# MLP and FFN up products by Strassen's seven products, down products over 512 features at a time

## The chip, the cores and the metric

One core of one Trainium2 chip runs the whole program: 512 tokens, 1024 features, all data and products in 32 bits. The metric is the device time of one execution in microseconds (us). The engines are TensorE (PE, its weight loads apart as PEld), VectorE (DVE), ScalarE (ACT), GpSimd (POOL) and SyncE (SP, which here issues the DMAs). Each runs its own instructions in a fixed order and waits on semaphores for the others. Products end up in PSUM, in banks of 128 x 512; everything else lies in SBUF.

## The reference

Two layers of a first block, then one layer of a second. What the change touches are the two feed-forward parts; attention, convolution and mLSTM parts stay as they are.

```
# first block, for l in 0, 1 (hidden 4096)
u = rmsnorm(x, norm_mlp[l])
x = x + square(relu(u @ w_mlp_up[l])) @ w_mlp_down[l]
# second block, once (hidden 2816)
h = modulate(rms_norm(x, g_ffn), sh_f, sc_f)
x = x + gt_f * ((silu(h @ w_gate) * (h @ w_up)) @ w_down)
```

The vector `mod` (shifts, scales, gates) is a product of `w_ada` with one vector; the kernel computes it on DVE during layer 1's MLP.

## The kernel before

All activations lie transposed: eight tiles `x[j]` of 128 features x 512 tokens. A product is made to nearly full 32-bit precision out of three matmuls of type fp32r: every weight and activation is split into a high part (`hi`, a cast on ACT) and a low part (`lo`, a subtraction on DVE), and hi x hi, hi x lo and lo x hi add up in one PSUM bank (L230, L231, L232).

`Prog` (L48) holds the program as a list: a "unit" is a piece of weights of 128 x 4 x 256 (`split`, L164: ACT's cast L171, DVE's subtraction L172), a "do" is anything else, "bg" is background work of which `rate` pieces follow each unit. A unit's split is written two units ahead of its matmuls. The tile layer then orders each engine's instructions by its own estimate of times, so that rows of neighbouring steps mix. The pools `whp` (4 buffers each for `wh` and `wl`), `rawp` (3 buffers of 1 MB for weights as they come), `gp` (60 slots of 128 x 512, tag g) and `mmp` (4 PSUM banks, tag mm) set when a buffer comes free.

`linear` (L188) makes four output tiles from weights of 1024 x 512: for each unit, for each of its two tiles, 4 x 3 matmuls of 512 columns (tokens); at `parts_=2` twice as many of 256 columns. After the last one `evac` reads the bank: L732 (relu and scale on DVE), L733 (square on ACT) and `hilo` (L285, L286) for an up tile, L740 (addition to x) for a down tile.

In each layer's MLP `up(c)` makes 1024 of 4096 hidden features and `down(c)` takes them back, in the order up 0, up 1, down 0, up 2, down 1, up 3, down 2, down 3. Ahead of it, `evmix` (L715) adds each tile of the mixing product to x and `prep` (L289) makes the tile's `hi` and `lo`. In layer 1 the 96 ada products (L803, DVE, on SBUF data) are background work. `fin` (L881) makes the next norm for the first half of the tokens while the second part of the last down group runs. In the FFN `gateup(c, g)` makes two gate and two up tiles together (L1315 to L1317), eleven times, and `down(c)` takes 1024 features. `hnorm` (L843) makes its normed input, half the tokens at a time.

## Time and profile before

| | us |
|---|---|
| median of 3 runs | 2070.45 |
| lowest, highest | 2070.16, 2070.49 |
| the profiled execution | 2069.96 |
| its span | 2067.9 |

| engine | busy, share of the span | instructions |
|---|---|---|
| PE | 2057.1 us, 99% | 9944 |
| DVE | 1260.0 us, 61% | 2245 |
| ACT | 845.6 us, 41% | 1359 |
| POOL | 19.7 us, 1% | 33 |

The profile is of one execution. The span runs from its first instruction to its last; the time outside it belongs to the execution too. Matmuls overlap, so a busy PE says that something was always in it, not how fast; their pace is read from start to start. An average over the whole span hides that the stages have different loads: layer 0's MLP lies at about 325 to 715 us, layer 1's at 1040 to 1435, the FFN from 1690 to the end.

### The profile page before, as it was taken

The numbers are of one execution on the slowest core, as the hardware profiler recorded it, in microseconds if no ns is written. First come the engines' busy times: TensorE is split into PE (matmuls) and PEld (weight loads), VectorE is DVE, ScalarE is ACT, GpSimd is POOL, SyncE is SP. The second block draws the span as 40 slices with busy tenths as digits, with TensorE's granted clock in tenths as the row PEclk, the third lists the DMA queues.
The fourth block names the chain that finished last, engine by engine and source line by source line (L and its number), as shares of the span: only waits on it lengthen the run. The fifth ranks groups of instructions, "written<-read, shape, count | busy, mean of one in ns | idle before, by whom it ended". The sixth has DMA issues, their size and how long they took to land.

```text
span 2067.9 us, 25080 instructions
## 1 busy us (share of the span) xinstructions
PE 2057.1 (99%) x9944; PEld 1700.7 (82%) x9944; DVE 1260.0 (61%) x2245; ACT 845.6 (41%) x1359; POOL 19.7 (1%) x33
## 2 busy tenths in 40 slices
...
GB/s 204 102 94 93 79 62 102 82 102 102 96 88 102 87 94 90 102 102 62 62 123 169 209 141 194 145 195 98 82 82 62 42 81 103 81 103 101 83 111 51
DMA packets 122148, 215.25 MB, mean 104 GB/s; under 512 B 5808, under 2 KB 30640, under 8 KB 122032
## 3 DMA queue, kind: packets, MB, share of 16 engines
...
## 4 chain that ended last, share of the span: by engine, by line
PE 97%; DVE 1%; ACT 1%; issue 0%; DMA 0%; POOL 0%; SPq 0%; POOLq 0%; DVEq 0%; ACTq 0%
PE mm L230 25%; PE mm L232 25%; PE mm L231 25%; PE mm L1315 4%; PE mm L1317 4%; PE mm L1316 4%; PE at L352 1%; PE mm L260 1%; PE mm L261 1%; PE mm L262 1%; PE ot L386 1%; PE at L371 1%; PE at L1188 0%; PE at L1196 0%; PE at L582 0%
## 5 line engine op out<-in xcount | busy, mean ns | idle before, releaser
L230 PE MATMUL mm<-g,wh 128*128 128x512 f32 (+1 forms) x2400 | 919.5, 384 | 1.0 <-ACT wh L171 0.8
L232 PE MATMUL mm<-g,wl 128*128 128x512 f32 (+1 forms) x2400 | 916.0, 382 | 0.0
L231 PE MATMUL mm<-g,wh 128*128 128x512 f32 (+1 forms) x2400 | 915.4, 382 | 0.0
L171 ACT CAST wh<-raw 128x1024 fp32r<-128x1024 f32 (+2 forms) x356 | 366.4, 1032 | 825.8 <-PE mm L231 648.6
L172 DVE TENSOR_TENSOR wl<-raw,wh 128x1024 fp32r<-128x1024 f32 (+2 forms) x356 | 424.9, 1195 | 448.1 <-ACT wh L171 445.8
L230 PEld LDWEIGHTS mm<-g,wh 128*128 128x128 f32 x2400 | 450.4, 188 | 90.5 <-issue 4.3
L231 PEld LDWEIGHTS mm<-g,wh 128*128 128x128 f32 x2400 | 450.6, 188 | 86.3 <-issue 1.2
L232 PEld LDWEIGHTS mm<-g,wl 128*128 128x128 f32 x2400 | 450.7, 188 | 86.1
L1317 PE MATMUL mm<-g,wl 128*128 128x512 f32 (+1 forms) x384 | 142.6, 372 | 0.0
L1316 PE MATMUL mm<-g,wh 128*128 128x512 f32 (+1 forms) x384 | 142.4, 372 | 0.0
L1315 PE MATMUL mm<-g,wh 128*128 128x512 f32 (+1 forms) x384 | 142.2, 372 | 0.0
L286 DVE TENSOR_TENSOR g<-g,g 128x512 fp32r<-128x512 f32 x96 | 66.4, 691 | 49.7 <-ACT g L285 49.2
L285 ACT CAST g<-g 128x512 fp32r<-128x512 f32 x96 | 59.6, 621 | 60.6 <-DVE g L707 26.6
L1317 PEld LDWEIGHTS mm<-g,wl 128*128 128x128 f32 x384 | 72.3, 188 | 12.6
L1316 PEld LDWEIGHTS mm<-g,wh 128*128 128x128 f32 x384 | 72.3, 188 | 12.5
L1315 PEld LDWEIGHTS mm<-g,wh 128*128 128x128 f32 x384 | 72.1, 188 | 12.4
L740 DVE TENSOR_TENSOR x<-mm,x 128x512 f32<-128x512 f32 (+1 forms) x68 | 44.8, 658 | 56.5 <-PE mm L232 56.5
L803 DVE SCALAR_TENSOR_TENSOR g<-g,g 128x512 f32<-128x512 f32 x96 | 63.8, 688 | 8.6 <-DMA g<-w_ada 8.5
L733 ACT ACTIVATE g<-g 128x512 f32<-128x512 f32 x64 | 40.3, 630 | 70.1 <-DVE g L732 70.1
L360 ACT ACTIVATE g<-g,nm 128x128 f32<-128x128 f32 (+3 forms) x96 | 53.2, 555 | 17.8 <-DVE nm L355 17.1
L601 DVE MAX8 m<-g 128x8 f32<-128x256 f32 (+2 forms) x96 | 53.3, 558 | 1.9
L602 DVE MATCH_REPLACE8 g<-m,g 128x256 f32<-128x256 f32 (+2 forms) x96 | 52.1, 543 | 0.0
...
## 6 DMA issues: line engine op xcount, KB each, us to landing
raw<-w_in SPq DMA_DIRECT2D x53, 1024.0 KB, 5.0
raw<-w_mlp_up SPq DMA_DIRECT2D x32, 1024.0 KB, 5.4
raw<-w_mlp_down SPq DMA_DIRECT2D x32, 1024.0 KB, 5.1
...
raw<-w_gate SPq DMA_DIRECT2D x11, 1024.0 KB, 5.1
raw<-w_up SPq DMA_DIRECT2D x11, 1024.0 KB, 5.2
raw<-w_down SPq DMA_DIRECT2D x10, 1024.0 KB, 5.0
raw<-w_mix_out SPq DMA_DIRECT2D x8, 1024.0 KB, 5.1
```

Of the source, the lines that this page charges most:

```text
L171: act.copy(hi, raw)
L172: dve.tensor_sub(lo, raw, hi.bitcast(F32))
L230: pe.matmul(ps, wh, hi[:, cs], start=st, stop=False)
L231: pe.matmul(ps, wh, lo[:, cs], start=False, stop=False)
L232: S["pe"] = pe.matmul(ps, wl, hi[:, cs], start=False, stop=en)
L285: act.copy(hi, src)
L286: dve.tensor_sub(lo, src, hi.bitcast(F32))
L601: dve.max(m8, acc[i][:, :W_])
L803: dve.scalar_tensor_tensor(w, w, 1.0, S["cb", n2], op0=ALU.mult, op1=ALU.mult, accum_out=modp[:, n2, n : n + 1])
L1315: pe.matmul(ps, wh, hi[:, cs], start=s == 0 and k_ == 0, stop=False)
L1316: pe.matmul(ps, wh, lo[:, cs], start=False, stop=False)
L1317: pe.matmul(ps, wl, hi[:, cs], start=False, stop=s == 1 and k_ == 3)
```

## The change

A unit of four output tiles (two column halves of 256, called 0 and 1) is now made by `strassen`. It halves K (tiles 0 to 3 and 4 to 7), the columns and the tokens, and makes seven products of half-size matrices in place of eight. Each is a unit of 128 x 4 x 256 weights with 2 x 4 x 3 matmuls of 256 columns. They add up in four banks, X, Z, Y and V, and additions out of the banks put them together (`keep`, `e11` to `e21`); X, Z and V are read while later products still go into them. Sums and differences of weights (tag ws, a new pool of 3 buffers) are made on GpSimd by `combine`, those of activations (`ta`, `tb`) by `mix`, also on GpSimd, and then split by `hilo`. `whp` has 3 buffers instead of 4. Up units make 512 hidden features (8 a layer, 10 in the FFN, where column half 0 is gate and 1 is up; the FFN's first group stays as it was), and each down product takes 512 features, with half as many matmuls and as many additions to x. Rope tables come by DMA into slots, and no longer lie in `kon`. The rate of the ada work is 0.65 per unit instead of 0.8.

```diff
-K_RES = 1408
+K_RES = 384
...
-    whp = ctx.enter_context(tc.tile_pool(name="whp", bufs=4))
+    whp = ctx.enter_context(tc.tile_pool(name="whp", bufs=3))
+    ssp = ctx.enter_context(tc.tile_pool(name="ssp", bufs=3))
...
     def split(u):
-        chunk, k0, kn, cc0, ccn = u["src"]
-        if id(chunk) not in raws:
-            raws[id(chunk)] = fetch(chunk)
-        raw = raws[id(chunk)][:, k0 : k0 + kn, cc0 : cc0 + ccn]
+        if "make" in u:
+            raw = u["make"]()
...
+    def strassen(srcs, xs, ta, tb, evac):
+        raw = {}
+        sums = {}
+        bank = {}
+        tmp = {}
+        def A(n, r):
+            if r not in raw:
+                raw[r] = rawp.tile([P, 4, 512], F32, tag="raw", name=nm("raw"))
+                rows = slice(512 * r, 512 * (r + 1))
+                (W0, c0), (W1, c1) = srcs
+                if W0 is W1 and c1 == c0 + 256:
+                    nc.sync.dma_start(raw[r], W0[rows, c0 : c0 + 512].rearrange("(k p) c -> p k c", p=P))
+                else:
+                    nc.sync.dma_start(raw[r][:, :, 0:256], W0[rows, c0 : c0 + 256].rearrange("(k p) c -> p k c", p=P))
+                    nc.sync.dma_start(raw[r][:, :, 256:512], W1[rows, c1 : c1 + 256].rearrange("(k p) c -> p k c", p=P))
+            return raw[r][:, :, 256 * n : 256 * n + 256]
+        def combine(name, f, a_, b_):
+            sums[name] = ssp.tile([P, 4, 256], F32, tag="ws", name=nm("ws"))
+            f(sums[name], a_, b_)
+        def w11():
+            A(0, 0), A(0, 1)
+            combine(1, pool.tensor_add, A(1, 0), A(1, 1))
+            combine(3, pool.tensor_sub, A(0, 0), A(1, 0))
+            return A(0, 0)
+        def w1():
+            combine(2, pool.tensor_sub, sums[1], A(0, 0))
+            return sums[1]
+        def w12():
+            combine(4, pool.tensor_sub, A(0, 1), sums[2])
+            return A(0, 1)
+        def half(d, k0, t):
+            return lambda k: [o[:, th(t)] for o in d(k0 + k)]
+        prods = [
+            ("X", w11, half(xs, 0, 0)),
+            ("Z", w1, half(ta, 0, 0)),
+            ("X", w12, half(xs, 4, 0)),
+            ("Z", lambda: sums[4], half(xs, 4, 1)),
+            ("Y", lambda: sums[2], half(tb, 0, 0)),
+            ("V", lambda: sums[3], half(ta, 0, 1)),
+            ("V", lambda: A(1, 1), half(tb, 0, 1)),
+        ]
+        def keep(name):
+            def f():
+                tmp[name] = slot()
+                act.copy(tmp[name], bank[name])
+            return f
+        def e11():
+            evac(0, 0, bank.pop("X"), False)
+        def e12():
+            u = tmp["U"] = slot()
+            dve.tensor_add(u, bank.pop("Y"), tmp.pop("X"))
+            r = slot()
+            dve.tensor_add(r, bank.pop("Z"), u)
+            evac(0, 1, r, True)
+        def e22():
+            u = slot()
+            dve.tensor_add(u, bank["V"], tmp["U"])
+            pool.tensor_add(u, u, tmp.pop("Z"))
+            evac(1, 1, u, True)
+        def e21():
+            r = tmp.pop("U")
+            dve.tensor_add(r, bank.pop("V"), r)
+            evac(1, 0, r, True)
+        after = [keep("X"), keep("Z"), e11, None, e12, e22, e21]
+        pieces = []
+        for n, (b, make, mv) in enumerate(prods):
+            u = {"make": make}
+            first = b not in [q[0] for q in prods[:n]]
+            last = b not in [q[0] for q in prods[n + 1 :]]
+            for m in range(2):
+                def emit(u=u, b=b, mv=mv, m=m, first=first, last=last):
+                    if first and m == 0:
+                        bank[b] = mmbank()
+                    ps = bank[b][:, th(m)]
+                    for k in range(4):
+                        hi, lo = mv(k)
+                        wh = u["hi"][:, k, m * P : (m + 1) * P]
+                        wl = u["lo"][:, k, m * P : (m + 1) * P]
+                        pe.matmul(ps, wh, hi, start=first and m == 0 and k == 0, stop=False, skip_group_check=True)
+                        pe.matmul(ps, wh, lo, start=False, stop=False, skip_group_check=True)
+                        S["pe"] = pe.matmul(ps, wl, hi, start=False, stop=k == 3, skip_group_check=True)
+                pieces.append(([("unit", u)] if m == 0 else []) + [("do", emit)])
+            if after[n]:
+                pieces[-1].append(("do", after[n]))
+        return pieces
...
+        if mixed:
+            y = S[key, "y", j] = slot()
+            pool.tensor_scalar(y, x[j], gcol, None, op0=ALU.mult)
+            mix(key, j)
...
+    def mix(key, j):
+        if j < 4:
+            t = S[key, "ta", j] = slot()
+            y = S[key, "y", j]
+            pool.tensor_sub(t[:, th(0)], y[:, th(1)], y[:, th(0)])
+            return
+        k = j - 4
+        a_, b_ = S[key, "ta", k], slot()
+        y0, y1 = S.pop((key, "y", k)), S.pop((key, "y", j))
+        pool.tensor_sub(b_[:, th(0)], y1[:, th(1)], a_[:, th(0)])
+        pool.tensor_sub(a_[:, th(1)], y1[:, th(1)], y0[:, th(1)])
+        pool.tensor_sub(b_[:, th(1)], y1[:, th(0)], b_[:, th(0)])
+        S[key, "ta", k] = hilo(a_)
+        S[key, "tb", k] = hilo(b_)
...
+        def rope_tables():
+            for n, o in (("Cr", K_RC), ("Sr", K_RS)):
+                S[n] = slot()
+                nc.sync.dma_start(S[n], a["const"][:, o : o + T])
...
-                prep("n", j, col(C_NMLP + 8 * l + j))
+                prep("n", j, col(C_NMLP + 8 * l + j), mixed=True)
...
+        def evup(c):
+            def f(n, t, src, own):
+                r = src if own else slot()
+                dve.scalar_tensor_tensor(two(r), two(src), 0.0, both(S["n", "rs"][:, th(t)]), op0=ALU.max, op1=ALU.mult)
                 S["act"] = act.activation(r, r, AF.Square)
-                hid[c, 4 * g + j] = hilo(r)
+                for m in range(2):
+                    k_ = 4 * c + 2 * n + m
+                    if k_ not in hid:
+                        hid[k_] = (slot(F32R), slot(F32R))
+                    hi, lo = hid[k_]
+                    act.copy(hi[:, th(t)], r[:, th(m)])
+                    dve.tensor_sub(lo[:, th(t)], r[:, th(m)], hi[:, th(t)].bitcast(F32))
...
+            W_ = a["w_mlp_up"][l]
+            return strassen([(W_, 512 * c), (W_, 512 * c + 256)], xs, lambda k: S["n", "ta", k], lambda k: S["n", "tb", k], evup(c))
...
+                p += linear(a["w_mlp_down"][l], 512 * c, [4], 512 * g, [P] * 4, lambda k: hid[4 * c + k], evdn(c, g),
+                            parts_=2 if l == 1 and c == NU - 1 and g == 1 else 1)
...
-            I.append(("rate", 0.8))
+            I.append(("rate", 0.65))
...
+        for c in range(1, NU):
+            add(up(c))
+            if c == NU - 1:
+                do(freen)
+                I.append(("drain", None))
+            add(down(c - 1))
...
+            if mixed:
+                if cs.start == 0:
+                    S[key, "y", j] = slot()
+                pool.tensor_scalar(S[key, "y", j][:, cs], t[:, cs], b, None, op0=ALU.add)
...
+        def unit(c):
+            gt = {}
+            def evac(n, t, src, own):
+                if n == 0:
+                    gt[t] = src if own else slot()
+                    act.activation(gt[t], src, AF.Silu)
+                    return
+                r = gt.pop(t)
+                dve.tensor_mul(r, src, r)
+                for m in range(2):
+                    k_ = 2 * c + m
+                    if k_ not in ff:
+                        ff[k_] = (slot(F32R), slot(F32R))
+                    hi, lo = ff[k_]
+                    act.copy(hi[:, th(t)], r[:, th(m)])
+                    dve.tensor_sub(lo[:, th(t)], r[:, th(m)], hi[:, th(t)].bitcast(F32))
+            return strassen([(a["w_gate_2"], 256 * c), (a["w_up_2"], 256 * c)], xs, lambda k: S["h", "ta", k],
+                            lambda k: S["h", "tb", k], evac)
...
+                p += linear(a["w_down_2"], 512 * c, [kt], 512 * g, [P] * 4, lambda k_: ff[4 * c + k_], evff(c, g))
...
+        def ffn_mix():
+            for j in range(KT):
+                mix("h", j)
...
+        u0 = gateup()
         add(u0[:8])
         do(lambda: S.pop("rest")())
+        do(ffn_mix)
         add(u0[8:])
-        add(up(1))
-        add(down(0))
-        add(up(2))
-        add(down(1))
-        add(down(2))
+        for c in range(1, NG):
+            add(unit(c))
+            if c % 2 == 0:
+                add(down(c // 2 - 1))
+        add(down(ND - 1))
```

Three places in the order. First PE, in layer 0's MLP. Before, where one up tile ends and the next begins (mm is a bank, wh and wl the weights' parts, g the activations):

```order
L230 MATMUL mm_734_3318<-g_694_3112,wh_715_3227 128x512
L231 MATMUL mm_734_3318<-g_695_3113,wh_715_3227 128x512
L232 MATMUL mm_734_3318<-g_694_3112,wl_716_3228 128x512
L230 MATMUL mm_735_3331<-g_684_3050,wh_715_3227 128x512
L231 MATMUL mm_735_3331<-g_685_3051,wh_715_3227 128x512
L232 MATMUL mm_735_3331<-g_684_3050,wl_716_3228 128x512
```

Now, where the sixth product (bank mm_882, V) ends and the seventh follows:

```order
L358 MATMUL mm_882_4188<-g_754_3347,wh_872_4115 128x256
L359 MATMUL mm_882_4188<-g_755_3348,wh_872_4115 128x256
L360 MATMUL mm_882_4188<-g_754_3347,wl_873_4116 128x256
L238 MATMUL mm_893_4267<-g_812_3718,wh_880_4184 128x512
L239 MATMUL mm_893_4267<-g_813_3719,wh_880_4184 128x512
L240 MATMUL mm_893_4267<-g_812_3718,wl_881_4185 128x512
L238 MATMUL mm_893_4267<-g_814_3722,wh_880_4184 128x512
L239 MATMUL mm_893_4267<-g_815_3723,wh_880_4184 128x512
L240 MATMUL mm_893_4267<-g_814_3722,wl_881_4185 128x512
L358 MATMUL mm_882_4188<-g_726_3243,wh_874_4143 128x256
L359 MATMUL mm_882_4188<-g_727_3244,wh_874_4143 128x256
L360 MATMUL mm_882_4188<-g_726_3243,wl_875_4144 128x256
```

Six matmuls of a down tile (mm_893) have moved between two products that go into the same bank.

Second, DVE at the start of layer 0's MLP, from the last addition to x on. Before:

```order
L718 TENSOR_TENSOR x7_99<-mm_705_3168,x7_99 128x512
L172 TENSOR_TENSOR wl_733_3315<-raw_723_3271,wh_732_3314 128x1024
L294 SCALAR_TENSOR_TENSOR g_721_3265<-x7_99,cols_85,g_720_3264 128x512
L307 TENSOR_TENSOR g_53_312<-g_53_312,g_722_3268 128x512
L172 TENSOR_TENSOR wl_738_3347<-raw_736_3344,wh_737_3346 128x1024
L316 TENSOR_SCALAR g_730_3306<-at_728_3303 128x512
L317 RECIPROCAL g_731_3307<-g_729_3305 128x512
L323 TENSOR_TENSOR g_729_3305<-g_731_3307 128x512
```

Now (L413 is `hilo` of ta and tb, L421 is `prep`, L454 the squares' sum):

```order
L870 TENSOR_TENSOR x7_102<-mm_712_3188,x7_102 128x512
L413 TENSOR_TENSOR g_734_3274<-g_691_3085,g_733_3273 128x512
L180 TENSOR_TENSOR wl_760_3358<-raw_714_3203,wh_759_3357 128x1024
L413 TENSOR_TENSOR g_736_3278<-g_732_3269,g_735_3277 128x512
L421 SCALAR_TENSOR_TENSOR g_741_3301<-x6_101,cols_88,g_740_3300 128x512
L180 TENSOR_TENSOR wl_768_3400<-ws_758_3355,wh_767_3399 128x1024
L454 TENSOR_TENSOR g_55_319<-g_55_319,g_742_3304 128x512
L413 TENSOR_TENSOR g_746_3314<-g_698_3113,g_745_3313 128x512
L413 TENSOR_TENSOR g_748_3318<-g_744_3309,g_747_3317 128x512
L421 SCALAR_TENSOR_TENSOR g_750_3335<-x7_102,cols_88,g_749_3334 128x512
L454 TENSOR_TENSOR g_55_319<-g_55_319,g_751_3338 128x512
L413 TENSOR_TENSOR g_755_3348<-g_703_3137,g_754_3347 128x512
```

and POOL in the same stretch, where no row stood before (L427 is y, L440 to L442 `mix`, L286 a sum of weights):

```order
L427 TENSOR_SCALAR g_743_3307<-x6_101,cols_88 128x512
L440 TENSOR_TENSOR g_744_3309<-g_743_3307,g_698_3113 128x256
L441 TENSOR_TENSOR g_698_3113<-g_743_3307,g_697_3111 128x256
L442 TENSOR_TENSOR g_744_3309<-g_743_3307,g_744_3309 128x256
L286 TENSOR_TENSOR ws_787_3540<-raw_785_3536,raw_786_3538 128x1024
L427 TENSOR_SCALAR g_752_3341<-x7_102,cols_88 128x512
L440 TENSOR_TENSOR g_753_3343<-g_752_3341,g_703_3137 128x256
L441 TENSOR_TENSOR g_703_3137<-g_752_3341,g_702_3135 128x256
L442 TENSOR_TENSOR g_753_3343<-g_752_3341,g_753_3343 128x256
L286 TENSOR_TENSOR ws_788_3542<-raw_785_3536 128x1024
L286 TENSOR_TENSOR ws_797_3586<-ws_787_3540,raw_785_3536 128x1024
L286 TENSOR_TENSOR ws_800_3623<-raw_786_3538,ws_797_3586 128x1024
```

The subtractions of ta and tb and the weights of the next products have moved in ahead of the reciprocal (L317 before, L464 now).

Third, DVE in the FFN. Before, in the gate and up tiles (L1326 is the product of gate and up, L1331 `hilo`):

```order
L172 TENSOR_TENSOR wl_2957_14783<-raw_2945_14712,wh_2956_14782 128x1024
L1331 TENSOR_TENSOR g_2951_14749<-g_2944_14710,g_2950_14748 128x512
L172 TENSOR_TENSOR wl_2962_14815<-raw_2960_14812,wh_2961_14814 128x1024
L172 TENSOR_TENSOR wl_2967_14849<-raw_2965_14846,wh_2966_14848 128x1024
L172 TENSOR_TENSOR wl_2973_14887<-raw_2960_14812,wh_2972_14886 128x1024
L1326 TENSOR_TENSOR g_2963_14830<-mm_2958_14786,g_2963_14830 128x512
L1331 TENSOR_TENSOR g_2969_14866<-g_2963_14830,g_2968_14865 128x512
L1326 TENSOR_TENSOR g_2964_14844<-mm_2959_14799,g_2964_14844 128x512
L172 TENSOR_TENSOR wl_2977_14917<-raw_2965_14846,wh_2976_14916 128x1024
```

Now, at the end of the first of two units in a row (L326 and L328 are `e12`, L333 `e22`, L339 `e21`, L1507 the product, L1514 the low parts):

```order
L180 TENSOR_TENSOR wl_3346_17152<-raw_3319_16956,wh_3345_17151 128x1024
L326 TENSOR_TENSOR g_3348_17180<-mm_3347_17155,g_3335_17060 128x512
L328 TENSOR_TENSOR g_3349_17182<-mm_3338_17066,g_3348_17180 128x512
L180 TENSOR_TENSOR wl_3355_17196<-raw_3350_17185,wh_3354_17195 128x1024
L333 TENSOR_TENSOR g_3357_17224<-mm_3356_17199,g_3348_17180 128x512
L180 TENSOR_TENSOR wl_3364_17239<-ws_3352_17191,wh_3363_17238 128x1024
L1507 TENSOR_TENSOR g_3349_17182<-g_3357_17224,g_3349_17182 128x512
L1514 TENSOR_TENSOR g_3359_17229<-g_3349_17182,g_3358_17228 128x256
L1514 TENSOR_TENSOR g_3361_17233<-g_3349_17182,g_3360_17232 128x256
L339 TENSOR_TENSOR g_3348_17180<-mm_3356_17199,g_3348_17180 128x512
L1507 TENSOR_TENSOR g_3342_17121<-g_3348_17180,g_3342_17121 128x512
L180 TENSOR_TENSOR wl_3367_17275<-raw_3351_17188,wh_3366_17274 128x1024
```

and POOL there, where no row stood before (L334 is the addition in `e22`):

```order
L286 TENSOR_TENSOR ws_3326_16995<-ws_3320_16959,raw_3318_16953 128x1024
L286 TENSOR_TENSOR ws_3331_17029<-raw_3319_16956,ws_3326_16995 128x1024
L286 TENSOR_TENSOR ws_3352_17191<-raw_3350_17185,raw_3351_17188 128x1024
L286 TENSOR_TENSOR ws_3353_17193<-raw_3350_17185 128x1024
L286 TENSOR_TENSOR ws_3362_17236<-ws_3352_17191,raw_3350_17185 128x1024
L334 TENSOR_TENSOR g_3357_17224<-g_3357_17224,g_3339_17091 128x512
L286 TENSOR_TENSOR ws_3365_17272<-raw_3351_17188,ws_3362_17236 128x1024
```

The last addition out of V (L339) and the split for the next unit's third product (wl_3367) now stand behind a product that waits for POOL.

## Rows read from the trace of the kernel before

**Rows 1.** The page: engines' busy time, and the chain's shares by engine.
```profile
PE 2057.1 (99%) x9944; PEld 1700.7 (82%) x9944; DVE 1260.0 (61%) x2245; ACT 845.6 (41%) x1359; POOL 19.7 (1%) x33
...
PE 97%; DVE 1%; ACT 1%; issue 0%; DMA 0%; POOL 0%; SPq 0%; POOLq 0%; DVEq 0%; ACTq 0%
```

**Rows 2.** Waits of PE: line waited for, us in total, times, longest.
```profile
PE at L371 <- DVE nm L355: 2.0, 3, 0.9
...
PE mm L230 <- ACT wh L171: 0.8, 1, 0.8
```

**Rows 3.** Timeline, layer 0's MLP (start, duration, engine, line, tiles), 23 matmuls left out.
```profile
500.01 0.39 PE L230 MATMUL mm<-g,wh 128*128 128x512 f32 x1
...
505.45 0.39 PE L230 MATMUL mm<-g,wh 128*128 128x512 f32 x1
```

**Rows 4.** Timeline, two-part output projection, PE; 89 matmuls left out.
```profile
1679.84 0.28 PE L230 MATMUL mm<-g,wh 128*128 128x256 f32 x1
...
1690.64 0.28 PE L230 MATMUL mm<-g,wh 128*128 128x256 f32 x1
```

**Rows 5.** Busy us by engine: MLP of layer 0, of layer 1, FFN.
```profile
core 0: us, PE busy (x) PEld busy (x) DVE busy (x) ACT busy (x) POOL busy (x), PEclk, DMA share, GB/s
...
480.00:520.00 40.00, 40.00 (x178) 33.11 (x178) 16.10 (x18) 12.02 (x15) 0.00 (x0) 1.00 0.32 101
1100.00:1140.00 40.00, 40.00 (x178) 33.15 (x177) 27.68 (x51) 15.88 (x22) 0.00 (x0) 1.00 0.54 184
1800.00:1840.00 40.00, 40.00 (x178) 33.14 (x177) 13.94 (x15) 11.84 (x15) 0.00 (x0) 1.00 0.27 85
```

**Rows 6.** Groups by line and shape: count, busy us, mean ns, idle before.
```profile
L232 PEld LDWEIGHTS mm<-g,wl 128*128 128x128 f32 x2384 | 448.5, 188 | 84.7
...
L172 DVE TENSOR_TENSOR wl<-raw,wh 128x1024 fp32r<-128x1024 f32 x342 | 417.5, 1222 | 436.5 <-ACT wh L171 434.2 <-PE at L313 0.7
L171 ACT CAST wh<-raw 128x1024 fp32r<-128x1024 f32 x342 | 359.6, 1053 | 802.8 <-PE mm L231 627.4 <-PE mm L1316 81.0 <-issue 71.4
...
L803 DVE SCALAR_TENSOR_TENSOR g<-g,g 128x512 f32<-128x512 f32 x96 | 63.8, 688 | 8.6 <-DMA g<-w_ada 8.5
...
L732 DVE SCALAR_TENSOR_TENSOR g<-mm,g 128x512 f32<-128x512 f32 x64 | 44.2, 690 | 7.2 <-PE mm L232 7.0
L740 DVE TENSOR_TENSOR x<-mm,x 128x512 f32<-128x512 f32 x60 | 41.4, 690 | 52.7 <-PE mm L232 52.7
...
L863 DVE SCALAR_TENSOR_TENSOR g<-g,modc,g 128x256 fp32r<-128x256 f32 x32 | 14.5, 480 | 0.8 <-ACT g L860 0.8
...
L317 DVE RECIPROCAL g<-g 128x512 f32<-128x512 f32 x4 | 13.4, 3344 | 0.0
```

**Rows 7.** DMA issues: KB each, median us to landing.
```profile
raw<-w_mlp_up SPq DMA_DIRECT2D x32, 1024.0 KB, 5.4
```

**Rows 8.** Timeline, layer 0's attention, two places, PE and ACT left out.
```profile
231.93 0.42 DVE L355 CUSTOM_DVE_ANT_0 g<-at,bias 128x256 f32<-128x256 f32 x1
231.96 0.61 POOL L412 CAST g<-g 64x512 fp32r<-64x512 f32 x1 [1.33 <-DVE g L411]
...
262.48 0.68 DVE L411 TENSOR_TENSOR g<-g,g 64x512 fp32r<-64x512 f32 x1
...
263.20 0.69 DVE L403 TENSOR_TENSOR g<-g,g 64x512 fp32r<-64x512 f32 x1
263.30 1.06 POOL L412 CAST g<-g 64x512 fp32r<-64x512 f32 x1 [15.12 <-DVE g L411]
...
263.92 0.99 DVE L411 TENSOR_TENSOR g<-g,g 64x512 fp32r<-64x512 f32 x1
```

**Rows 9.** Timeline: the last matmul of a tile, its relu product.
```profile
510.66 0.39 PE L232 MATMUL mm<-g,wl 128*128 128x512 f32 x1
...
511.09 0.69 DVE L732 SCALAR_TENSOR_TENSOR g<-mm,g 128x512 f32<-128x512 f32 x1 [0.64 <-PE mm L232]
```

101 lines of the change are left out of this document (48 added, 53 removed).

## The prediction

> **What bounds the kernel now.** I read the page's engine line and its chain first: TensorE (PE) is busy for 99% of 2067.9 us and holds 97% of the chain that ended last [rows 1]. Then what PE waited for: the longest sum is 2.0 us in all [rows 2]. So the time is PE's stream of matmuls, plus 2.06 us outside the span (2069.96 - 2067.9); the median of three runs, 2070.45, is 0.5 above the profiled execution, against which I sum. A change pays if it shortens that stream and loses less through new waits of PE.
>
> Next the price of a matmul, from start to start, since durations (0.39 and 0.28 us) overlap. Of 512 columns, 24 steps take 505.45 - 500.01 = 5.44 us, 0.2267 each [rows 3]; of 256 columns, 90 steps take 1690.64 - 1679.84 = 10.80, 0.1200 each [rows 4]. Half the columns cost 53%, not 50%. Last, the helpers: in up and down stages VectorE (DVE) is busy 16.1 of 40 us in layer 0, 27.7 in layer 1 with the ada products and 13.9 in the FFN; GpSimd (POOL) is idle [rows 5].
>
> **The gain.** I number the seven products of a unit P1 to P7 in the order of their code: P1 and P3 add up in bank X, P2 and P4 in Z, P5 in Y, P6 and P7 in V. Four output tiles took 4 x 8 x 3 = 96 matmuls of 512: 21.76 us. A unit takes 7 x 2 x 4 x 3 = 168 of 256: 20.16. That is 1.60 less. There are 8 units in each of two layers and 10 in the FFN: 26 x 1.60 = 41.6. The down products keep their matmuls, but for the last two-part group of layer 1, which is half as deep: 192 x 0.1200 = 23.0 becomes 96 x 0.1200 + 48 x 0.2267 = 22.4. Together **-42.2 us**. At a pitch of 21.76 / 168 = 0.1295 nothing would be left of it.
>
> **What DVE and POOL get.** One up unit and the down half behind it give PE 20.16 + 21.76 = 41.9 us. DVE's part by durations of [rows 6]: 11 weight splits x 1.22, 4 additions that put the products together, 4 relu products and 8 x additions, all x 0.69, and 8 half-width subtractions x 0.48: 28.3 us. ScalarE (ACT) has 11 x 1.05 and small casts, some 20, and is no bound. The split's buffers go from four to three: a split can begin when the product before the running one is done, which leaves two products, 5.8 us, for 1.05 + 1.22; enough unless DVE is behind, and then PE waits for it at once. Weights still come in pieces of 1 MB, 5.4 us each [rows 7], through three buffers; a unit's two pieces are asked for while the down half before it is split, over 10 us ahead of their use. I cost that at nothing; the down half is the cover, and without it a unit would lose up to 5.4. The rope tables, two more transfers of 256 KB a layer in SP's queue against 512 KB less of the constants, are first used after the first group of products: nothing.
>
> POOL gets four weight sums of 1024 elements and one addition of 512. The trace has no two-input POOL operation. Its CAST takes 0.61 us for 512 elements [rows 8]; a sum writes twice that and reads four times: 1.2 to 2.4 us. I take 2.4 (1.2 for 512, 0.6 for 256), since every operand has to be read; 10.8 us a unit. The Trainium skill (GPSIMD Engine Reference, section Performance versus the Vector engine) has 4497 ns for an addition of 2048 elements, so 2.25 us here as an estimate; no run here shows it, and by it the sum below falls some 3 us.
>
> **Do they run side by side?** At 263.30 the CAST met a DVE subtraction of two SBUF tensors: it took 1.06 instead of 0.61, and the next such subtraction 0.99 instead of 0.68. The three took 264.91 - 263.20 = 1.71 us against 1.98 one after another. At 231.96 the CAST ran beside DVE work on PSUM and took 0.61 [rows 8]. So the two take turns where DVE reads two SBUF tensors, as splits, half-width subtractions and ada products all do, and not on the sums out of PSUM. The Trainium skill (SBUF — State Buffer, section Who interferes with whom) says the same: whichever starts first holds the shared pair of ports for its whole instruction, which speaks against putting sums on GpSimd here; the trace agrees (0.45 us lost by a 0.61 us CAST).
>
> **Where PE will wait.** All estimates, from the counts in the new order and durations of [rows 6, 8, 9].
>
> (1) Between P6 and P7 DVE must read V, which P7 overwrites by adding. DVE started 0.43 us after the last 512-column matmul started (0.04 after its end) [rows 9]; for 256 columns 0.28 + 0.04, then 0.69 and a wake-up of 0.05: P7 can start 1.06 after P6's last start. The order puts six down matmuls in between in layer 0 (0.12 + 1.36 = 1.48) and eight matmuls of the next unit or four of a down product in the FFN (1.08, 1.03). DVE comes to it 0.2 to 0.3 late in layer 0 (two additions, a split, a relu product after P5: 3.3 us against a product's 2.88 and the same start delay). Covered: 0 to 0.3 each, **1 us** over 26. Without these filling matmuls it would be 1 us each.
>
> (2) At the start of each MLP, P2 needs ta, so the x addition of the last tile, three POOL operations, an ACT cast and a DVE subtraction; P2 is due 2.9 us in. From that addition to the V sum of the second unit DVE has 13 splits, 28 operations x 0.69, 10 x 0.48 and a reciprocal of 3.34 [rows 6]: 43.3 us, where PE has 13 products, 37.4. At least 5.9 are lost. POOL's four sums, two tiles of mixing (4 x 0.6 each) and two additions, 17 us, come in turns with that: at most 23. I take 15. In layer 1, 14 ada products x 0.69 stand in the same stretch: 15.6 to 33, **25**; together **40**. Before, this place had a whole unit of ordinary products as cover.
>
> (3) Layer 1, the other units: DVE 28.3 + 14 x 0.69 = 38.0, with POOL's 10.8 in turns 48.8, less the 12 operations on PSUM (8.3) that can pass beside POOL: 40.5 to 48.8 against 41.9. 0 to 6.9 each; I take 2, nearer the low end, since up to 19 filling matmuls stand before P7. Six such units: **12**. Layer 0, without ada, stays below 39: 0 (to 2 each).
>
> (4) FFN, two units in a row, five times. Three buffers hold sums; the second unit's first sum waits for the first unit's P6 split, which waits for P3's weights to come free: 8.64 + cast 1.05 + split 1.22 = 11 us in. Then POOL has three sums, V's addition and the fourth sum. In turns with splits at 12.8 and 16.0 the third sum ends near 20.5; P2's split, V's addition and the fourth sum bring it to 25.3; a product, two half subtractions, the last V addition, a product and P3's split end DVE's row at 29.6. PE, 0.5 late at P7, is at the second unit's P3 at 26.4. So 3.6 a pair, **18**; without turns 0, at worst 25.
>
> (5) At the FFN's start the same mixing has half of the first gate/up group as cover: POOL has 28 operations of 0.6. I take **5** (0 to 10). (6) The final norm's chain in layer 1 has half its old cover (5.8 us instead of 11.5): **2** (0 to 4).
>
> Sum: -42.2 + 1 + 40 + 12 + 18 + 5 + 2 = +35.8; 2069.96 + 35.8 = **2106 us**.
>
> **The rivals.** (A, faster) A POOL sum costs 1.2 us and seldom meets a split. Then DVE's own load alone is left: 5.9 + 15.6 at the starts, 1, 2 and 2 for (1), (5), (6): -42.2 + 26.5, so **2054**. For it: POOL's sums stand mostly in down stages, where DVE is half idle [rows 5]. Against it: [rows 8], and that a sum reads two tensors. It decides at a POOL sum of some 1.5 us, where the fourth sum of (4) comes in time. (B, faster) The order hides everything: -42.2 + 1, **2029**; against it the 43.3 against 37.4 in (2), which needs no POOL. (C, slower still) The turns bind DVE in all of layer 1: 41 in (3), 23 + 33 at the starts, 25 in (4): up to +80 + 10; taken at half way to that, **2140**. For it: 48.8 against 41.9. Against it: DVE waits for ACT anyway in each unit, and POOL can use those gaps. (D) The pitch of 256-column matmuls is not 0.1200 in a product whose weights change with each split; weights load in 188 ns beside the matmuls in [rows 6] at either width, so I give it little; at 0.13 it would eat the gain, 2150.
>
> **How the numbers follow.** Forecast, 2066 to 2125 about 2106: 0.51; A, 2042 to 2066 about 2054: 0.26; B 0.05, C 0.15, D 0.03. What this measurement can tell from no change is 0.2%, 4 us: 2066 to 2074. Faster is A and B less a little of A's upper tail: 0.29. Same: 0.07, from A's upper and the forecast's lower tail. Slower: the rest, 0.64. The range for 8 in 10 runs from A's lower end to C: 2042 to 2140.
>
> **What would show it.** PE's waits should name DVE weight splits (the wl tiles) and the ta halves, most at the two MLP starts, then the second units of FFN pairs; 256-column starts 0.12 apart between waits; POOL sums near 2.4 us, longer where a split runs; splits of 1.22 stretched to 2 or 3. Wrong at once: PE waits below 30 us in all (A or B), or POOL sums near 1.2. The granted clock is 1.00 in these stretches [rows 5], where PE never pauses; that it could fall after pauses of several us is not in the sum, and would add to it.

## The result, and the profile after

The changed kernel takes 2176.52 us (median of four runs, 2175.94 to 2180.48) where the kernel before takes 2070.3: a ratio of 1.0518, 95% interval 1.050 to 1.0536. The forecast was 2106, the range 2042 to 2140. The sign is right, the size is not: 106 us slower instead of 36, outside the range. The profiled execution has a span of 2175.2 us, 107.3 more than before.

The page of after first, the rows that answer to [rows 1] (engines' busy time), then two of its rows in 40 slices (POOL busy, and the granted clock, 9 for full speed):

```profile
PE 2062.0 (95%) x11768; PEld 1777.3 (82%) x11768; DVE 1656.7 (76%) x2623; ACT 967.0 (44%) x1597; POOL 434.7 (20%) x243
...
POOL 0000006333222000000263222310010016333440
PEclk9999999799999999999989999999999997999999
```

PE's share has fallen from 99 to 95%, POOL has gone from 19.7 us to 434.7, and there are slices in which TensorE's clock is below full speed. Before there was none. The waits of PE, as in [rows 2] (line waited for, us in total, times, longest):

```profile
PE mm L238 <- DVE x L899: 21.3, 11, 3.6
PE mm L358 <- ACT g L1484: 16.2, 1, 16.2
PE mm L358 <- ACT g L412: 12.4, 4, 3.4
PE mm L359 <- DVE g L413: 9.4, 4, 4.3
PE mm L360 <- DVE wl L180: 8.8, 8, 1.7
...
PE mm L387 <- DVE g L655: 3.7, 2, 3.2
```

All lines of that answer together are 108.5 us; before they were 6.7. So waits explain 102, and the gain of 42 has to be paid too: 107.3 + 42.2 = 149.5 us were lost, 47 more than the waits. By PE's steps (below), 34 of the 47 are in steps at a lower clock, 6 in steps that end a wait (a wait counts from the modelled end of the matmul ahead, later than its pitch), 6 in short delays. Stretches of 25 us (us busy and number of instructions of PE, weight loads, DVE, ACT, POOL, then granted clock, DMA share, GB/s), to be set against [rows 5]:

```profile
375.00:400.00 25.00, 12.57 (x61) 9.94 (x62) 19.66 (x19) 12.83 (x18) 15.31 (x14) 0.66 0.00 0
1100.00:1125.00 25.00, 12.61 (x62) 9.72 (x61) 19.66 (x20) 11.78 (x17) 17.67 (x14) 0.66 0.13 43
...
1825.00:1850.00 25.00, 14.71 (x106) 14.71 (x107) 16.49 (x16) 9.86 (x16) 13.98 (x10) 0.71 0.00 1
```

At both MLP starts (375, 1100) and the FFN's (1825) PE has 61, 62 and 106 matmuls in 25 us instead of the 110 of 512 columns or 208 of 256 that fit, and the clock is at its lower level (1.2 GHz, 0.5) for part of the stretch. The mean over the execution is 0.977 (1.000 before), so it stood there for (1 - 0.977) x 2 x 2175 = 100 us, a part of them with PE paused. The products themselves cost what was forecast; from the timeline in layer 0's first unit, nine rows left out:

```profile
371.73 0.28 PE L358 MATMUL mm<-g,wh 128*128 128x256 f32 x1
...
372.93 0.28 PE L359 MATMUL mm<-g,wh 128*128 128x256 f32 x1
```

Ten steps in 1.20 us, 0.1200 each, as in [rows 4].

To place the loss, I took for every matmul of PE the step to the next one's start, less 0.2267 us (512 columns) or 0.1200 (256), and summed it by stretch, for after and for before. The difference is what was lost there, waits and slow clock together (steps of other shapes are not in it):

| stretch of after | us lost | of it waits | forecast, with its number |
|---|---|---|---|
| up to layer 0's MLP (to 365 us) | 5.4 | 2.6 | 0 |
| start of layer 0's MLP (365 to 430) | 26.5 | 17.9 | 15 (2) |
| rest of it (to 790) | 4.8 | 3.4 | 1 (1) |
| start of layer 1's MLP (1092 to 1162) | 27.2 | 19.7 | 25 (2) |
| rest of it (to 1490) | 30.2 | 19.2 | 12 (3) |
| final norm, second block's first part (to 1771) | 8.7 | 4.5 | 2 (6) |
| start of the FFN (1771 to 1846) | 33.6 | 25.5 | 5 (5) |
| rest of the FFN | 12.6 | 9.3 | 18 (4) |
| sum | 149.0 | 102.1 | 78 |

149.0 less the gain of 42.2 is 106.8, against the 107.3 measured. Layer 1's attention (790 to 1092) lost nothing.

### The profile page after: what moved, and what is told of

It is laid out like the page before. It is cut to its first block, busy times and chain, and to the rows that moved or that the text cites. A ratio compares the mean times of both kernels' runs of the same rounds, so it can differ in the third digit from the quotient of the medians.

```text
span 2175.2 us, 29860 instructions
## 1 busy us (share of the span) xinstructions
PE 2062.0 (95%) x11768; PEld 1777.3 (82%) x11768; DVE 1656.7 (76%) x2623; ACT 967.0 (44%) x1597; POOL 434.7 (20%) x243
## 4 chain that ended last, share of the span: by engine, by line
PE 74%; DVE 15%; POOL 4%; issue 4%; ACT 3%; POOLq 0%; ACTq 0%; DVEq 0%
PE mm L238 16%; PE mm L239 16%; PE mm L240 16%; PE mm L358 6%; PE mm L359 6%; PE mm L360 6%; DVE wl L180 4%; DVE g L893 3%; DVE g L961 2%; ACT wh L179 2%; PE at L499 1%; PE ot L533 1%; PE at L518 1%; PE mm L387 1%; PE mm L388 1%
## 5 line engine op out<-in xcount | busy, mean ns | idle before, releaser
L238 PE MATMUL mm<-g,wh 128*128 128x512 f32 (+2 forms) x1872 | 722.8, 387 | 24.0 <-DVE x L899 21.3
L240 PE MATMUL mm<-g,wl 128*128 128x512 f32 (+2 forms) x1872 | 718.3, 384 | 0.5 <-DVE wl L180 0.5
L239 PE MATMUL mm<-g,wh 128*128 128x512 f32 (+2 forms) x1872 | 718.6, 384 | 0.0
L179 ACT CAST wh<-raw 128x1024 fp32r<-128x1024 f32 (+1 forms) x330 | 337.9, 1028 | 577.5 <-PE mm L239 415.5
L180 DVE TENSOR_TENSOR wl<-raw,wh 128x1024 fp32r<-128x1024 f32 (+1 forms) x330 | 444.2, 1348 | 120.3 <-ACT wh L179 117.9
L358 PE MATMUL mm<-g,wh 128*128 128x256 f32 x1456 | 419.3, 288 | 42.8 <-ACT g L1484 16.2
L238 PEld LDWEIGHTS mm<-g,wh 128*128 128x128 f32 (+1 forms) x1872 | 354.3, 190 | 99.4 <-issue 27.6
L359 PE MATMUL mm<-g,wh 128*128 128x256 f32 x1456 | 417.0, 287 | 9.7 <-DVE g L413 9.4
L360 PE MATMUL mm<-g,wl 128*128 128x256 f32 x1456 | 415.7, 286 | 8.8 <-DVE wl L180 8.8
L240 PEld LDWEIGHTS mm<-g,wl 128*128 128x128 f32 (+1 forms) x1872 | 354.6, 189 | 68.2 <-DVE wl L180 0.7
L239 PEld LDWEIGHTS mm<-g,wh 128*128 128x128 f32 (+1 forms) x1872 | 354.7, 190 | 66.0 <-issue 0.7
L358 PEld LDWEIGHTS mm<-g,wh 128*128 128x128 f32 x1456 | 283.7, 195 | 53.0 <-ACT g L1484 16.4
L359 PEld LDWEIGHTS mm<-g,wh 128*128 128x128 f32 x1456 | 283.8, 195 | 12.2 <-DVE g L413 11.2
L360 PEld LDWEIGHTS mm<-g,wl 128*128 128x128 f32 x1456 | 283.2, 195 | 10.5 <-DVE wl L180 10.5
L334 POOL TENSOR_TENSOR g<-g,g 128x512 f32<-128x512 f32 x26 | 51.5, 1981 | 381.4 <-DVE g L333 213.4
L286 POOL TENSOR_TENSOR ws<-raw,raw 128x1024 f32<-128x1024 f32 x26 | 71.4, 2746 | 118.1 <-DMA raw<-w_mlp_up 57.0
L286 POOL TENSOR_TENSOR ws<-raw,ws 128x1024 f32<-128x1024 f32 x26 | 65.1, 2505 | 121.3 <-DVE wl L180 102.2
```

Of the source, the lines that this page charges most:

```text
L179: act.copy(hi, raw)
L180: dve.tensor_sub(lo, raw, hi.bitcast(F32))
L238: pe.matmul(ps, wh, hi[:, cs], start=st, stop=False)
L239: pe.matmul(ps, wh, lo[:, cs], start=False, stop=False)
L240: S["pe"] = pe.matmul(ps, wl, hi[:, cs], start=False, stop=en)
L286: f(sums[name], a_, b_)
```

## Three places in the trace

**POOL's operations.** Groups by line and shape, as in [rows 6] (count, busy us, mean ns, idle before): weight sums, the addition in `e22`, the scaled copy y of the mix (in the MLPs, then in the FFN by halves):

```profile
L286 POOL TENSOR_TENSOR ws<-raw,raw 128x1024 f32<-128x1024 f32 x26 | 71.4, 2746 | 118.1 <-DMA raw<-w_mlp_up 57.0 <-DVE wl L180 34.6 <-DMA raw<-w_up 26.5
...
L286 POOL TENSOR_TENSOR ws<-raw,ws 128x1024 f32<-128x1024 f32 x26 | 65.1, 2505 | 121.3 <-DVE wl L180 102.2 <-issue 19.1
L334 POOL TENSOR_TENSOR g<-g,g 128x512 f32<-128x512 f32 x26 | 51.5, 1981 | 381.4 <-DVE g L333 213.4 <-ACT wh L179 151.2 <-ACT g L886 16.8
L427 POOL TENSOR_SCALAR g<-x,cols 128x512 f32<-128x512 f32 x16 | 31.8, 1988 | 150.8 <-DVE x L870 150.8
...
L1025 POOL TENSOR_SCALAR g<-g,modc 128x256 f32<-128x256 f32 x16 | 16.3, 1026 | 134.3 <-DVE g L1008 133.1 <-PE mm L240 1.2
```

Two groups of DVE, from the same view:

```profile
L180 DVE TENSOR_TENSOR wl<-raw,wh 128x1024 fp32r<-128x1024 f32 x316 | 436.9, 1384 | 114.0 <-ACT wh L179 111.6
...
L893 DVE TENSOR_TENSOR g<-g,g 128x256 fp32r<-128x256 f32 x128 | 104.6, 842 | 9.0 <-ACT g L892 9.0
```

A sum of 1024 elements takes 2.5 to 2.75 us, a little above the upper bound of 2.4 that I took. The estimate that the prediction worked out from the Trainium skill (GPSIMD Engine Reference, section Performance versus the Vector engine), 2.25, is below it. The addition of 512 elements in `e22`, priced at 1.2, takes 1.98. The scaled copy y, which I had priced at 0.6 like the CAST of [rows 8] (on 64 partitions instead of 128), takes 1.99 for 512 elements and 1.03 for 256. DVE's own operations have grown: the mean split from 1.22 to 1.38, the half-width subtraction of `evup`, priced at 0.48, to 0.84; the medians are 1.22 and 0.42, and single ones are several times longer (up to 3.43 and 2.63).

**Layer 1, where those two meet.** The timeline of after, 1266 to 1276 us, POOL (start, duration, engine, line, tiles):

```profile
1266.99 2.93 POOL L286 TENSOR_TENSOR ws<-raw,raw 128x1024 f32<-128x1024 f32 x1 [4.29 <-DMA raw<-w_mlp_up]
1269.88 2.59 POOL L286 TENSOR_TENSOR ws<-raw 128x1024 f32<-128x1024 f32 x1
1272.43 2.58 POOL L286 TENSOR_TENSOR ws<-ws,raw 128x1024 f32<-128x1024 f32 x1
```

DVE in the same timeline, to 1281 us:

```profile
1268.18 4.57 DVE L893 TENSOR_TENSOR g<-g,g 128x256 fp32r<-128x256 f32 x2
1272.68 2.88 DVE L961 SCALAR_TENSOR_TENSOR g<-g,g 128x512 f32<-128x512 f32 x1
...
1276.11 1.22 DVE L180 TENSOR_TENSOR wl<-raw,wh 128x1024 fp32r<-128x1024 f32 x1
1277.24 0.68 DVE L961 SCALAR_TENSOR_TENSOR g<-g,g 128x512 f32<-128x512 f32 x1
...
1277.85 0.68 DVE L961 SCALAR_TENSOR_TENSOR g<-g,g 128x512 f32<-128x512 f32 x1
...
1278.46 1.28 DVE L899 TENSOR_TENSOR x<-mm,x 128x512 f32<-128x512 f32 x2
1279.67 1.21 DVE L180 TENSOR_TENSOR wl<-raw,wh 128x1024 fp32r<-128x1024 f32 x1
1280.80 0.68 DVE L899 TENSOR_TENSOR x<-mm,x 128x512 f32<-128x512 f32 x1
```

PE in it, 1279 to 1281 us:

```profile
1279.29 0.47 PE L238 MATMUL mm<-g,wh 128*128 128x512 f32 x1 [3.65 <-DVE x L899]
...
1280.65 0.63 PE L239 MATMUL mm<-g,wh 128*128 128x512 f32 x1
1281.08 0.63 PE L240 MATMUL mm<-g,wl 128*128 128x512 f32 x1
```

Three sums follow one another on POOL for 8.0 us. In that time DVE finishes two half-width subtractions (4.57 us, 0.76 elsewhere) and begins one ada product (2.88, 0.68 elsewhere): it gets in only between two sums. Once POOL is done, three more ada products (the first at 1275.49) and a split still stand ahead in DVE's row. The addition to x that frees a bank comes at 1278.46, and PE has waited 3.65 us for it. Then its clock is at 1.2 GHz: 512-column matmuls 0.43 us apart. Such waits come five times, 2.45 us once and 3.6 four times, some 47 us apart (and one of 1.41 us ahead of them).

**The start of the FFN.** The timeline of ACT in after, 1826 to 1836 us:

```profile
1826.84 1.14 ACT L412 CAST g<-g 128x512 fp32r<-128x512 f32 x2 [2.72 <-POOL g L442]
1832.38 1.14 ACT L412 CAST g<-g 128x512 fp32r<-128x512 f32 x2 [4.40 <-POOL g L442]
...
1834.86 0.65 ACT L1484 ACTIVATE g<-mm 128x256 f32<-128x256 f32 x2
```

and of PE:

```profile
1835.29 0.58 PE L358 MATMUL mm<-g,wh 128*128 128x256 f32 x1 [16.22 <-ACT g L1484]
```

PE's first Strassen product needs a bank which the SiLU of the ordinary group (L1484) still has to read. That SiLU stands in ACT's row behind the casts of ta and tb (L412), which wait for POOL's mix. PE waits 16.2 us. POOL's own row there holds 32 operations of y and mix, 31.8 us of work, and between them the four weight sums of the first Strassen unit, another 10.8.

## Experiments

Each kernel is the changed one with the edit shown; each of the last three builds on the run described ahead of it. Times are single runs, except the last kernel's; before took 2069.7 to 2070.6 on the same chip each time.

**The mix left out.** ta and tb are plain inputs; 80 operations of POOL (the expectation says 68), with their casts and subtractions, are gone.

```diff
+    def mix(key, j):
+        if j >= 4:
+            S[key, "ta", j - 4] = S[key, j - 4]
+            S[key, "tb", j - 4] = S[key, j - 4]
```

> The changed kernel without the mixing of activations: ta and tb are the plain normed inputs, so GpSimd's 68 mixing operations, their casts and their subtractions are left out (that part of the computation is not done). In the changed kernel the three starts lose most: by start-to-start steps against 0.1200 and 0.2267 us, 26.5 us more than before at layer 0's MLP (360 to 430 us), 27.6 at layer 1's (1095 to 1165) and 33.5 at the FFN's (1770 to 1850). Theory (POOL's mixing chain ends last there, and the fallen clock follows its waits): nearly all of these 87.6 go, 5 or less stay at each start: 2176 - 75 = 2100 us. Rival (DVE's own list at the start, 43.3 us of it against 37.4 of products, as the forecast had it): with the 16 subtractions of the mix gone 35 to 38 stay against 37.4, but the sums of weights come in turns with them; some 10 stay at each start: 2120 or more.

2128.93 us. The starts lose 12.0, 13.1 and 17.4 instead of 26.5, 27.2 and 33.6: half of the loss goes, half stays: nearer to the rival's number. So the mix is one cause there, and not the only one.

**The weight sums left out.**

```diff
-            sums[name] = ssp.tile([P, 4, 256], F32, tag="ws", name=nm("ws"))
-            f(sums[name], a_, b_)
+            sums[name] = a_
```

> The changed kernel without the sums and differences of weights on GpSimd: products are made with a plain piece of weights in their place (left out: those 104 operations), the mix of activations stays. Theory (a POOL operation on SBUF keeps DVE off its own SBUF operations for its whole length): layer 1's five waits of 2.5 to 3.6 us for an addition to x go, so its 30.2 us after the start fall under 8; the five pairs of 0.93 in the FFN go (12.4 to under 3); the starts keep their mixing but lose 10 us of POOL's list each, some 8 of their loss: 2176 - 22 - 10 - 24 = 2120 us. Rival (in layer 1 the DVE has too much with the ada products, whether or not POOL works): layer 1's 30 keep above 15, 2135 or more.

2114.52 us. Layer 1's rest loses 4.1 instead of 30.2, the FFN's rest 1.2 instead of 12.6, the starts 7 to 9 less each. With the ada products all still there, the waits of 3.6 us are gone: it takes POOL's sums to make them, as the theory had it, and DVE's own list alone does not.

**Half of the ada products in layer 0.**

```diff
-        if l == 1:
-            do(ada_start)
-            I.append(("rate", 0.65))
-            I.append(("bg", [ada(n) for n in range(48)] + [ada_end]))
+        do(ada_start)
+        I.append(("rate", 0.33 if l else 0.3))
+        I.append(("bg", [ada(n) for n in (range(24, 48) if l else range(24))] + [ada_end if l else ada_free]))
```

> The changed kernel with half of the 96 ada products moved into layer 0's MLP, at about 0.3 a unit in both layers instead of 0.65 in layer 1. DVE has some 7 products less a unit in layer 1 (4.8 us), and as many more in layer 0. Theory (DVE in turns with POOL is just over the 41.9 us of PE in layer 1, so 4.8 less is enough): the five waits of 3.6 and their fallen clock go, 30.2 to under 10, layer 1's start gains 3 to 6, layer 0 loses 0 to 6: about 2155 us. Rival (POOL's three sums in a row hold DVE for 8 us, and the tile behind them waits whatever else DVE has to do): the waits of some 3 us stay, 2172 or more.

2169.01 us, neither number. Layer 1's rest does fall as expected, 30.2 to 6.8, with POOL's sums all still there: the waits of 3.6 us need both, the sums and the full number of ada products in DVE's row. But layer 0's rest rises from 4.8 to 16.3, and both MLP starts by 3, where layer 1's was expected to gain. So most of the loss only moves: 23 us gained there, 18 lost in these three stretches. Why layer 0's rest loses 16.3 with seven ada products a unit and layer 1's only 6.8 is not shown.

**PE kept busy in the five waits.**

```diff
+    def fill(n):
+        b = atbank()
+        with tc.issue_after(S["pe"].ins):
+            for _ in range(n):
+                pe.matmul(b[:, :K_RES], ones, kon, start=True, stop=True)
```

called with 4 ahead of the seventh down tile of a layer-1 group, in five places.

> The changed kernel with four matmuls of 384 columns on constants (one row of PE, into a bank nobody reads) just ahead of the down tile that waits 2.5 to 3.6 us in five places of layer 1; they lie inside the wait and change nothing that is computed. Theory (the granted clock falls after PE has paused for some 2.5 us): with PE busy there the clock stays at 1.00 in the five places; 3.4 us at half clock each were 1.7 us lost: 2176 - 8.5 = 2168 us, the waits for the x additions end where they did. Rival (the clock falls for another reason, such as the work of the stretch): the same five falls, and 2176 us.

2171.17 us. The same place as above in this kernel's timeline, the filling matmuls (each shows as two) and the tile behind the wait:

```profile
1274.12 2.74 PE L266 MATMUL at<-kon 128*128 128x384 f32 x8
1277.93 0.47 PE L241 MATMUL mm<-g,wh 128*128 128x512 f32 x1 [1.07 <-DVE x L908]
1278.23 0.39 PE L242 MATMUL mm<-g,wh 128*128 128x512 f32 x1
```

a stretch of 4 us behind it, with the columns of the stretches above:

```profile
1278.00:1282.00 4.00, 4.00 (x18) 3.29 (x19) 4.00 (x10) 0.00 (x0) 0.00 (x0) 1.00 0.85 298
```

and the stretch behind the same wait in after:

```profile
1280.00:1283.00 3.00, 3.00 (x8) 2.33 (x8) 3.00 (x7) 0.00 (x0) 0.00 (x0) 0.50 0.78 281
```

PE still waits 1.07 us, but 4 us behind it hold 18 matmuls at a clock of 1.00, where after has 8 in 3 us at 0.50. All five falls are gone and layer 1 is 7.1 us shorter (8.5 forecast). So the clock falls because PE pauses, and most long pauses are paid for again behind it. The Trainium skill (TensorE: Matmul & The Clock Gate, section Why this matters for your kernels) has a rule against long idle gaps of PE between bursts of matmuls; this run agrees with it, 1.00 against 0.50.

Not every long pause is followed by a fall. In the run without the mix, PE waits as long in one of the same five places:

```profile
1250.77 0.47 PE L238 MATMUL mm<-g,wh 128*128 128x512 f32 x1 [3.64 <-DVE x L886]
```

and the stretch behind it holds 14 matmuls at full clock:

```profile
1250.90:1254.00 3.10, 3.10 (x14) 2.57 (x15) 3.10 (x6) 0.00 (x0) 0.00 (x0) 1.00 0.99 320
```

The other four were followed by half the clock.

**Four split buffers, 56 slots.**

```diff
-    gp = ctx.enter_context(tc.tile_pool(name="gp", bufs=60))
+    gp = ctx.enter_context(tc.tile_pool(name="gp", bufs=56))
-    whp = ctx.enter_context(tc.tile_pool(name="whp", bufs=3))
+    whp = ctx.enter_context(tc.tile_pool(name="whp", bufs=4))
```

> The changed kernel with four buffers for split weights as before (and 56 slots of 128 x 512 in place of 60, to make room). In the changed kernel PE waits 3.2 us at 61 us of layer 0 for a bank read by the 4-row product of DVE, and its clock then falls (1.7 us more); before, 18 matmuls of a third piece of weights stood between, which need a third free pair of buffers. Theory (the fourth buffer puts those matmuls back ahead of the wait): the 5.4 us more in layer 0's first part go; the rest of the kernel, where seven splits a unit follow one another, gains a few us at most from the deeper row: 2176 - 5 = 2171 us. Rival (buffers are what starves the splits behind P3 and P6, in the FFN's pairs and in layer 1): the 0.93 us waits in pairs and the 3.6 us waits of layer 1 go too, 2140 to 2150.

2156.00 us. The 3.2 us wait at 61 us goes with its slow clock (5.4 lost becomes 1.4). The rest gains some 16 us, spread thin (6 at the FFN's start, 4 in layer 1, 2 in the FFN): more than the theory's few, less than the rival's; the waits for x additions stay, if shorter (10.9 us in five).

**The FFN's mix behind its first group.**

```diff
-        do(ffn_mix)
         add(u0[8:])
+        do(ffn_mix)
```

> The changed kernel with one line moved: the mix for the FFN is written behind the second half of its first group instead of ahead of it, so that the SiLU of that half stands ahead of the casts of ta and tb in ScalarE's row. In the changed kernel PE waits 16.2 us at 1835 us for that SiLU, which holds a bank; the casts ahead of it wait for GpSimd. Theory (both the row and the length of the chain: the mix ends at about 1834 in any case, so the wait is divided, P1 of the first Strassen unit runs, and P2 then waits for ta): 3 to 6 us gained, a wait of 8 to 13 us for ta in its place: 2172 us. Rival (the row alone: without the casts ahead of it nothing waits long): the 16.2 us and some 5 of fallen clock go, 2155 us.

2174.74 us. The wait for the SiLU is gone, and in its place PE waits for ta, from 1790 to 1870 us:

```profile
PE mm L358 <- ACT g L412: 6.8, 3, 4.4
PE mm L359 <- DVE g L413: 6.4, 4, 2.9
```

13.2 for 16.2. The chain of the mix is as long as before, only someone else waits for it.

**Sums on DVE.** In `combine` and `e22`, dve for pool.

```diff
-            combine(1, pool.tensor_add, A(1, 0), A(1, 1))
+            combine(1, dve.tensor_add, A(1, 0), A(1, 1))
```

> The changed kernel with the sums of weights and the addition in e22 on VectorE instead of GpSimd; the mixing of activations stays on GpSimd. A sum should take 1.2 us there (the split of the same size does) instead of 2.4 to 2.75, and none of it can hold up a DVE instruction by surprise. DVE's list in layer 1 becomes 28.3 + 4 x 1.22 + 0.69 + 14 x 0.69 = 43.5 us against PE's 41.9. Theory (time in which the two engines exclude each other counts, so 5.6 us on DVE is cheaper than 11.6 on POOL): layer 1 after its start loses 7 x 1.7 = 12 instead of 30.2, the FFN's pairs under 5 instead of 12.4, the starts some 5 less each: 2176 - 18 - 8 - 15 = 2135 us. Rival (DVE is the scarce engine, and whatever is taken off it is gained, as the change has it): DVE's list grows by 5.6 a unit, layer 1 loses more than now, 2185 or more.

2124.34 us, better than expected. A sum costs DVE half of what it costs POOL; a group of this kernel:

```profile
L286 DVE TENSOR_TENSOR ws<-raw,raw 128x1024 f32<-128x1024 f32 x26 | 32.7, 1258 | 0.2
```

Layer 1's rest loses 0.9, the FFN's 1.2, layer 0's 0.9: DVE takes on 5.6 us a unit and PE waits less. The starts do not follow: 20.7, 28.7 and 30.4, a gain of 7.5 in all where 15 were expected. By my list of durations DVE had 43.5 us of work for 41.9. But durations overlap: in the timeline above, two additions at 1278.46 take 1.21 to the next start (0.61 each, 0.68 by duration), and the split at 1279.67 is followed at 1280.80, 1.13 for 1.21. By steps the list is about 39, an estimate from these two.

**Ordinary products first.** The first group of each MLP by `linear`, the FFN's second by `gateup`, with the evacuation of before.

```diff
-        u0 = up(0)
+        u0 = linear(a["w_mlp_up"][l], 0, [4, 4], 0, [P] * 4, xs, evup0)
```

> The changed kernel with the first 512 hidden features of each layer's MLP, and the FFN's second group of two gate and two up tiles, made by ordinary products as before; Strassen begins behind them. That costs 3 x 1.6 = 4.8 us of its gain. Theory (the starts lose because ta and tb are due 2.9 us into the first unit; with 21.8 us of ordinary products ahead the chain of the mix, some 20 us, is covered): the three starts' 87.6 us fall to 10 to 20, and 2176 - 72 + 5 = 2109 us. Rival (the list that DVE and POOL have to do at the start is as long as before, and only comes due later): half of the loss stays, 2137.

2161.89 us, worse than both numbers. A new wait of PE has taken the old one's place:

```profile
PE at L460 <- DVE g L454: 22.7, 2, 11.3
PE mm L1481 <- ACT g L1489: 15.8, 2, 13.8
```

L460 is the product of the squares' sum, 11.3 us late in each layer: the mix is written tile by tile ahead of the squares and stands ahead of them in the rows of ACT and DVE. Cover alone does not help work that stands in front of the cover's own helpers.

**All of it together**: ordinary products first, sums on DVE, ada in both layers, and besides y on ACT, half down products in the FFN, and the two-part group of layer 1 over 1024 features as before.

```diff
-            pool.tensor_scalar(y, x[j], gcol, None, op0=ALU.mult)
+            act.activation(y, x[j], AF.Copy, scale=gcol)
...
-            if c % 2 == 0:
-                add(down(c // 2 - 1))
+            if c >= 2:
+                add(down((c - 2) // 2, [c % 2]))
...
+            add(linear(a["w_mlp_down"][l], 512 * c, [4, 4], 512, [P] * 4, lambda k: hid[4 * c + k], evdn(NU - 1, 1), parts_=2))
```

> All together: ordinary products at the three starts, sums of weights on VectorE, half of the ada products in layer 0, the scaled inputs y of the mix on ScalarE instead of GpSimd, in the FFN one half of a down product behind each unit instead of a whole one behind two, and at the end of layer 1 the two-part group over 1024 features as before. Gain of the products: 42.2 - 4.8 - 0.6 = 36.8. Theory (every loss has its cause in the starts, in POOL's sums, in the ada products, or in the clock behind these waits): of the 150 us lost 15 to 35 stay (5 of them at the start of the program, which nothing here touches): 2048 to 2068 us, faster than before. Rival (256-column products, seven weight splits a unit and the additions make DVE's list too long in any arrangement): 2080 or more.

2106.90 us. Outside the starts 5 lost at the program's start, 3.4 at the end of layer 1, about 1 elsewhere; at the starts 15.1, 17.6 and 23.9. The rival's number, by the starts alone.

**The mix behind the squares.**

```diff
+        for n, p in enumerate(u0[2:]):
+            add([p])
+            for j in range(8)[2 * n - 2 : 2 * n] if n else ():
+                do(lambda j=j: ymix("n", j))
```

> As the run with everything together, but the mix of activations (y, ta, tb) is written behind the sum of squares, between the matmuls of the ordinary first group, in the FFN between those of the second; the ada products begin one unit later, at 0.4 a unit. In the run before it 15.5, 17.6 and 24 us were lost at the three starts (steps against 0.1200 and 0.2267): PE waited 3.8 us for the sum of squares, 3.6 for a bank that the late reciprocal kept, and in the FFN 8.0 and 4.7 for a SiLU that stood behind casts and copies of the mix in ScalarE's row. Theory (the loss left at the starts is the mix standing ahead of other work in the rows of ACT and DVE, not its own lateness): 5 to 8 stay at each start, 2107 - 35 = 2072 us, within 2062 to 2080. Rival (the mix only comes due later: P2 of the first Strassen unit then waits for it): the waits move to ta and tb, 2095 or more.

2096.45 us. The FFN's start is solved (23.9 to 5.8), the MLPs' are not: the wait is now for ta, as the rival had it.

PE's waits in this kernel:

```profile
PE mm L358 <- ACT g L412: 23.5, 8, 4.6
```

and ACT's own waits, 366 to 412 us:

```profile
ACT g L935 <- DVE g L934: 7.4, 3, 3.7
ACT g L412 <- POOL g L444: 7.0, 4, 2.0
```

ACT waits for POOL, POOL for y from ACT, DVE for ACT.

**Two ordinary groups and the first down product ahead**, and the four buffers. The ada products now begin with the third unit, at 0.45 a unit.

```diff
+        u0, u1 = [linear(a["w_mlp_up"][l], 0, [4, 4], 512 * c, [P] * 4, xs, evup0(c)) for c in range(2)]
...
+        for n, p in enumerate(u0[2:] + u1):
+            add([p])
+            if n in range(3, 11):
+                do(lambda j=n - 3: ymix("n", j))
+        add(down(0))
```

> As the run with the late mix, but two groups of each layer's MLP are ordinary products, the mix is written among the second, the first down product follows before Strassen begins; four buffers for split weights, 56 slots. Gain of the products 42.2 - 3 x 1.6 - 2 x 1.6 - 0.6 = 33.6. In the run with the late mix the waits at the MLP's starts were for ta (2.1, 3.2, 4.6, 1.9 us, with 24 us of fallen clock): y, the GpSimd operations, casts and subtractions pass one another between four engines, some 45 us from the sum of squares to the last ta. Theory (it is the length of that chain; 65 us of ordinary products cover it): 2 to 5 lost at each start, 6 in the FFN's, 4 at the end of layer 1, 2 in layer 0's first part, 4 elsewhere: 2070 - 34 + 26 = 2062 us, 2056 to 2068, faster than before. Rival (DVE has too much in the first 65 us whatever the order, so the waits of 15 to 20 a start stay): 2085.

2055.57 us, half a us below the range expected: faster than before. Two long waits of PE are left:

```profile
PE mm L238 <- DVE g L935: 11.0, 2, 5.7
```

**Casts of ta and tb one step behind POOL.**

```diff
+            j = n - 4
+            if j in range(8):
+                do(lambda j=j: ymix("n", j))
+            if j in range(5, 9):
+                do(lambda k=j - 5: mixed("n", k))
```

> As the run with two ordinary groups, but the casts and subtractions that split ta and tb are written one step behind the GpSimd operations that make them, and the steps begin one piece later. In the run before it PE waited once at each MLP's start, 5.3 and 5.7 us, for a product of relu and scale on DVE (with 6.8 us of fallen clock each); there each cast of ta stood in ScalarE's row 1.5 to 2.1 us waiting for GpSimd, with the square and casts of the ordinary tiles behind it. Theory (ScalarE's row, held up by GpSimd, holds up DVE and so the banks): the two waits and their fallen clock go: 2055.6 - 2 x 5.3 - 2 x 3.4 = 2038 us; 2036 to 2046, faster than before by over 1%. Rival (the steps later in the row make P2 wait for ta instead): a wait of 5 us or more for ta at each start, 2053 to 2065.

2045.92 us (median of four, 2044.94 to 2048.98), at the upper end of the range expected; ratio to before 0.9888, interval 0.9871 to 0.9904. Its page:

```profile
PE 2026.8 (99%) x11456; PEld 1744.1 (85%) x11456; DVE 1559.4 (76%) x2671; ACT 966.1 (47%) x1582; POOL 66.7 (3%) x81
...
PEclk9999999999999999999999999999999999999999
```

and PE's longest waits in it:

```profile
PE mm L238 <- DVE x L908: 3.8, 2, 1.9
PE mm L358 <- DVE g L333: 2.5, 3, 1.2
```

The gain forecast for the products is there (33.6 us with five ordinary groups); 24 of it arrive. Of the 9 that are lost 5 are waits (12.0 us in all against 6.7), none the clock. (The table below has 11.3 for this kernel: steps of the shapes that it leaves out are 3.4 us shorter here than before.)

What each run loses by stretch (us, as in the table above; time in the first column):

| run | us | to MLP 0 | start 0 | rest 0 | start 1 | rest 1 | norm | FFN start | FFN rest |
|---|---|---|---|---|---|---|---|---|---|
| after | 2176.5 | 5.4 | 26.5 | 4.8 | 27.2 | 30.2 | 8.7 | 33.6 | 12.6 |
| no mix | 2128.9 | 5.5 | 12.0 | 5.1 | 13.1 | 28.6 | 8.5 | 17.4 | 10.3 |
| no sums | 2114.5 | 6.9 | 17.5 | 1.0 | 19.6 | 4.1 | 10.3 | 26.1 | 1.2 |
| ada in both | 2169.0 | 4.4 | 29.6 | 16.3 | 30.2 | 6.8 | 7.1 | 33.4 | 12.6 |
| sums on DVE | 2124.3 | 6.4 | 20.7 | 0.9 | 28.7 | 0.9 | 7.2 | 30.4 | 1.2 |
| late mix | 2096.5 | 4.3 | 17.4 | 4.2 | 20.8 | 1.3 | 4.3 | 5.8 | 1.4 |
| staggered | 2045.9 | 1.1 | 0.0 | 3.4 | 2.1 | 3.8 | 0.4 | 0.0 | 0.5 |

## Why the prediction was wrong, point by point

**The gain** of 42.2 us was right: the pitch is 0.1200, and the losses less 42.2 give the measured time within 0.5. Rival D had no part in it.

**(1)** The V hand-over was right: in the whole kernel PE waits for a reading of V once, 3.06 us at the start of layer 1's MLP (L333), and nowhere in layer 0. The 4.8 us of layer 0's rest are mostly something else, five waits of 0.58 us for additions to x, which the sum did not have.

**(2)** The starts of the MLPs, forecast 40: their waits are 37.6, and with the clock behind them 53.7 were lost. The mechanism (ta and POOL's chain against 2.9 us) held: 21.8 us of the waits are for ta (L412, L413). That the sum of the waits came so near is in part luck. y takes 1.99 instead of 0.6, which makes the chain longer; DVE's list by durations, 43.3, is about 39 by steps; and the 10 us that the ada products were to add in layer 1 did not come: 17.9 and 19.7 us of waits in the two layers.

**(3)** Layer 1's other units, forecast 12: 30.2. The mechanism was there, the value was taken from the wrong end. I had bounds of 0 and 6.9 a unit, the low one because operations on PSUM could pass beside POOL, and took 2, because up to 19 filling matmuls stand before P7. The trace shows waits of 2.45 and four times 3.6, with 1.7 of clock behind each, and not at P7 but at a down tile: what DVE had next in its row was not on PSUM, and the addition to x that could have passed stood behind it.

**(4)** The FFN's pairs, forecast 18: 12.6, waits of 0.93 twice a pair, once for a split in the first unit's P7 and once at the second unit's P3, as forecast, but there for ACT's copy out of the bank (L318). **(6)** forecast 2, 8.7 with the clock.

**(5)** The start of the FFN, forecast 5, cost 33.6. This step failed outright. I named half of the first group as the cover of the mix and priced 28 POOL operations at 0.6, 17 us; there are 32, and they take 31.8, with four weight sums of 10.8 in the same row. And I did not ask what stands behind the casts of ta and tb in ACT's row: the SiLU that this very cover needs to give its banks back. The run with the mix behind the group shows that the row alone is not it either (13.2 us of waits stay): the chain over ACT, POOL and DVE is longer than its cover.

**Not in the sum.** The clock: 34 us, four fifths of the gain. The prediction named it in its last sentence and left it out, since in the trace of before PE does not pause in these stretches. A forecast that holds 78 us of waits had to carry it. And the fourth pair of split buffers: the prediction found three enough unless DVE is behind, and costed them at nothing. DVE was behind, and the run with four is 20.5 us shorter: 4.0 of the 5.4 lost at the program's start, where I had not asked, and the rest spread over the stretches of the table. These 20.5 lie within the losses listed above.

Waits were forecast at 78 and came to 102; with the 34 of the clock and the 13 around waits that is the miss of 71. Of the rivals, C (2140, POOL's turns bind layer 1) had the mechanism of (3), with 41 us for waits that came to 19.2, and even its full sum, 2160, would have been too low; A falls with the sums at 2.5 us and more.
